# Layer 2's output projection: two more row blocks by the seven-product scheme, and some low parts formed by adding transfers

## The chip, the core and the metric

The kernel runs on one NeuronCore of a Trainium2 chip. Its five engines work side by side: TensorE (PE, matrix products), VectorE (DVE), ScalarE (ACT), GpSimd (POOL) and SyncE (SP, which here only issues transfers). Weights and activations come from HBM by DMA. The metric is the device time of one execution in microseconds (us), the median of several runs.

## The reference, cut to what matters

A trunk of two layers works on 512 tokens of width 2048: a retention layer, then a latent-attention layer, then a final RMSNorm. All is float32. The change lies in the last product of layer 2 and what stands beside it:

```python
def mla_branch(h, pos, w_in, q_norm_g, w_uq, kv_norm_g, w_ukv, w_out):
    ...
    o = causal_block_attention(q, k, v).reshape(B, S, MLA_WIDTH)
    return (jax.nn.silu(g) * o) @ w_out        # (512, 2048) @ (2048, 2048)
...
        x = x + gate * y
    return rmsnorm(x, final_norm_g)
```

## The kernel before

**Layout.** The output is held transposed: 16 blocks `kt` of 128 output rows, each 512 tokens wide. The product runs over 2048 = 16 tiles of 128 input rows. To keep float32 accuracy every operand is split into a high part (a rounding to the matmul's type) and a low part (what is left), and each product is three matmuls: high by high, high by low, low by high. `split` (L134) does that: ScalarE copies with rounding, VectorE subtracts. `load_w` (L138) loads a weight unit into a raw buffer (tag `raw`, three buffers) and splits it into one of three pair buffers, taken in turn (`next_pair`, L231).

**Four stages of the output.** Stage r = 0 forms blocks 0 to 3 and stage r = 1 blocks 4 to 7, both plainly (L2540 to L2549): eight weight units each, a unit being two input tiles by 512 output columns, 24 matmuls of 512 columns. In the first five units of r = 0 lie the last two attention heads (`l2_hooks`, L2384). Then `seven` (from `seven_rows_steps`, L966) forms blocks 8 to 11 by a Strassen-Winograd scheme: inputs in an even and an odd tile, outputs in two pairs of blocks, tokens in two halves of 256, and seven products of half the inner length in place of eight. It has four steps of a first pass (products x, s, z, y) and four of a second (x, y, s); a product is 12 matmuls of 256 columns for each of them. Each step loads its even and odd weights, forms differences on VectorE (L1016 to L1019, L1030) and splits them. The sums of the activations that it multiplies come from `o2_sums` (L2408), for the input pairs u = 0 to 7, in two halves: "s" sums, used in the first pass, and "t" sums, used in the second. For u of 4 and more the t sums are split later by `o2_late_sums` (L2427). At last blocks 12 to 15 are done plainly (`last_load`, `last_prepare`, `last_product`), and the norm and the output follow.

**Evacuation.** `o2_put` (L2471) multiplies a block's sum by the gate, adds the residual that `o2_residual` (L2431) loaded (tag `pp`, five buffers), squares it and adds the squares up. Blocks 4 to 11 wait in the list `waiting`; `put_one` takes one out at set places (`work3`, L2573).

**Buffers and order.** Weights of `seven` and of the last stage are loaded into raw buffers that `turns3[0]` hands out in turn, the tag `raw` (three) and the tag `bw` (two). Their split parts lie in four buffers in turn (`seven_parts`, L2514). `behind(...)` (L463) puts what is written under it after the last instruction issued so far on the named engines: T_ is PE, V_ VectorE, A_ ScalarE, S_ SyncE's queue. Within that freedom a planner, working with assumed durations, fixes the order of each engine's instructions when the kernel is built; on the chip each engine then works in that order, and a waiting instruction holds up what is behind it. In the loop over `seven` (L2579) step j loads step j + 3 and the last stage's units (`loads3`), then the residual of block 4 + j; multiplies; forms late sums at j = 2 and 4; and prepares step j + 2.

Of the kernel before, what the change touches and what calls it, by code (L numbers as in the profile page):

```python
# [9 lines left out]
F32 = mybir.dt.float32  # L10
# [39 lines left out]
def hybrid_trunk_kernel(  # L50
# [59 lines left out]
    def aux(name):  # L110
        return psum.tile([P, T], F32, tag="aux", bufs=4, name=name)
# [22 lines left out]
    def split(src, hi, lo):  # L134
        ACT.copy(hi, src)  # L135
        DVE.tensor_sub(lo, src, hi.bitcast(F32))  # L136

    def load_w(parts, a, b, name, later=None, where=None, halved=False):  # L138

        raw = base.tile([P, a, b], F32, tag="raw", bufs=3, name=f"{name}_raw")  # L140
        for dst, src in parts:
            nc.sync.dma_start(dst(raw), src)
# [2265 lines left out]
    def o2_sums(u):  # L2408

        e, o = (o2_in[u][:, i, :] for i in range(2))  # L2410
        f0 = tmp(f"o2_s{u}f", (P, 2, H))
        if u < 4:
            f1 = tmp(f"o2_t{u}f", (P, 2, H))
        else:
            f1 = late_sums3[u] = l2_tile(*(("sg", 3) if u < 7 else ("rot", 2)), f"o2_t{u}f", (P, 2, H))
        DVE.tensor_add(f0[:, 0, :], e[:, H:], o[:, H:])
        DVE.tensor_sub(f0[:, 1, :], f0[:, 0, :], e[:, :H])
        DVE.tensor_sub(f1[:, 0, :], e[:, :H], e[:, H:])
        DVE.tensor_sub(f1[:, 1, :], o[:, :H], f0[:, 1, :])
        tag, bufs = ("big", 16) if u < 4 else ("k4", 8)  # L2420
        s = sums3[2 * u] = base.tile([P, 2, 2, H], F32R, tag=tag, bufs=bufs, name=f"o2_s{u}")
        split(f0, s[:, :, 0, :], s[:, :, 1, :])
        if u < 4:
            s = sums3[2 * u + 1] = l2_tile("pt", 4, f"o2_t{u}", (P, 2, 2, H), F32R)
            split(f1, s[:, :, 0, :], s[:, :, 1, :])

    def o2_late_sums(u):  # L2427
        s = sums3[2 * u + 1] = base.tile([P, 2, 2, H], F32R, tag="big", bufs=16, name=f"o2_t{u}")
        split(late_sums3.pop(u), s[:, :, 0, :], s[:, :, 1, :])

    def o2_residual(kt):  # L2431
        tag, bufs = ("sg", 3) if kt >= 13 else ("pp", 5)
        o2_res[kt] = l2p.tile([P, T], F32, tag=tag, bufs=bufs, name=f"o2_xr{kt}")
        nc.sync.dma_start(o2_res[kt], x1_d[kt * P : (kt + 1) * P, :])

    def o2_hooks(i):
        l2_hooks.get(i, lambda: None)()
        if i == 5:
            with behind(V_):
                gate_sum()  # L2440
        if 5 < i < 14 and sums3[2 * (i - 6)] is None:
            with behind(V_, A_):
                o2_sums(i - 6)
        if i in (13, 14, 15):
            with behind(S_):
                seven[i - 13].units[0][0]()
# [9 lines left out]
    with behind(V_):  # L2456
        scored(last[0])

    def o2_unit(r, u):
        with ExitStack() as stack:  # L2460
            for ins in o2_first if (r, u) in ((0, 1), (0, 2)) else ():
                stack.enter_context(tc.issue_after(ins))
            wt = load_w([(whole, rows(w_mla_out, u, 2, r * T, T))], 2, T, f"o2_w{r}_{u}")
        if u not in o2_hl:
            o2_parts(u)
        return wt
# [70 lines left out]
        lambda second, u: 0, ((False, 0),),  # L2537
    )

    for r in range(2):  # L2540
        run(
            chunk(
                [(lambda u=u: o2_unit(r, u), [2 * u, 2 * u + 1]) for u in range(KD // 2)],
                [(acc, aux)[r](f"o2_{r}_{b}") for b in range(4)],
                lambda w, ki, kt, b: w_block(w, ki, b), lambda w, ki, kt, b: o2_moving(kt),
                lambda b, ps: o2_out(b, ps)() if r == 0 else waiting.append(lambda: o2_out(4 + b, ps)()),
            ),
            each=lambda i: o2_hooks(r * (KD // 2) + i),
        )  # L2549
# [6 lines left out]
    def last_load(u):  # L2556
        last_raw[u] = turns3[0]([P, 2, T], f"o2_w3_{u}")
        nc.sync.dma_start(last_raw[u], rows(w_mla_out, u, 2, 3 * T, T))
# [16 lines left out]
        7: lambda: (put_one(), put_one(), last_prepare(2)),  # L2575
    }
    with behind(V_, A_):
        seven[1].units[0][1]()
# [207 lines left out]
```

## Time and profile before

| | |
|---|---|
| Median of three runs | 2115.03 us (2114.95 to 2115.57) |
| Profiled execution, its own time | 2114.73 us |
| Span of its trace | 2113.0 us |
| PE busy | 2098.4 us, 99% of the span |
| VectorE, ScalarE, GpSimd busy | 1680.8, 1054.1, 103.8 us |
| Stage r = 0 of the output | PE from about 1920 to 1973.4 us |
| Stage r = 1 | 1973.4 to 2016.9 us |
| `seven` | 2016.9 to 2055.3 us |
| Last blocks, norm, output | 2055.3 to 2113.0 us |

The span is the time from the first to the last instruction of the trace; the execution's own time adds 1.73 us around it. Busy time of PE is modelled and counts pipelined matmuls as overlapping, so the time that a row of matmuls takes is read from the starts of the first and of the next row. In group rows the columns are line, engine, operation, tile written and tiles read, shapes, count, then busy us, mean ns of one, and idle time before them with its cause. In rows in order of time the columns are start, duration, engine, line and operation; a bracket holds the idle time before it.

### The profile page before, as it was taken

The numbers are of one execution on the slowest core, as the hardware profiler recorded it, in microseconds if no ns is written. First come the engines' busy times: TensorE is split into PE (matmuls) and PEld (weight loads), VectorE is DVE, ScalarE is ACT, GpSimd is POOL, SyncE is SP. The second block draws the span as 40 slices with busy tenths as digits, with TensorE's granted clock in tenths as the row PEclk, the third lists the DMA queues.
The fourth block names the chain that finished last, engine by engine and source line by source line (L and its number), as shares of the span: only waits on it lengthen the run. The fifth ranks groups of instructions, "written<-read, shape, count | busy, mean of one in ns | idle before, by whom it ended". The sixth has DMA issues, their size and how long they took to land.

```text
span 2113.0 us, 30423 instructions
## 1 busy us (share of the span) xinstructions
PE 2098.4 (99%) x11268; PEld 1814.2 (86%) x11268; DVE 1680.8 (80%) x2562; ACT 1054.1 (50%) x1626; POOL 103.8 (5%) x177
## 2 busy tenths in 40 slices
PE   8999999999999999999999999999999999999998
PEld 6888898989889888888888888898889999888898
DVE  7999888888888789666777877767978788887675
ACT  6765444444444444434344445345446565665343
POOL 1001010000000000000000000010000000000000
PEclk9999999999999999999999999999999999999999
DMA  9975786868777778755656656753556655455453
GB/s 382 407 281 195 250 276 222 278 216 268 245 259 250 237 237 278 260 188 183 234 170 227 220 184 235 265 178 111 167 186 207 199 166 187 153 188 176 148 166 126
DMA packets 237303, 465.08 MB, mean 220 GB/s; under 512 B 21169, under 2 KB 91857, under 8 KB 233569
## 3 DMA queue, kind: packets, MB, share of 16 engines
q1 hardware_dynamic: 224512, 423.17, 60.5%
q0 software_dynamic: 11920, 38.91, 4.8%
q8 instruction: 88, 1.44, 0.3%
q10 hardware_dynamic: 722, 1.06, 0.2%
q14 instruction: 61, 0.50, 0.1%
HBM read 420.06 MB, written 43.00 MB: 219 GB/s over the span
## 4 chain that ended last, share of the span: by engine, by line
PE 95%; DMA 3%; DVE 1%; ACT 0%; SPq 0%; issue 0%; POOLq 0%; DVEq 0%
PE o L1486 16%; PE x L884 2%; PE x L883 2%; PE y L884 2%; PE y L883 2%; PE s L884 2%; PE s L883 2%; PE x L885 2%; PE s L885 2%; PE y L885 2%; PE o L2607 2%; PE qk L158 2%; PE s_qk L984 2%; PE x_qk L984 2%; PE qk L160 2%; PE qk L159 2%
## 5 line engine op out<-in xcount | busy, mean ns | idle before, releaser
L1486 PE MATMUL o<-o_h,o_p 128*128 128x512 f32 (+1 forms) x1088 | 322.9, 377 | 0.0
L1486 PEld LDWEIGHTS o<-o_h,o_p 128*128 128x128 f32 x1088 | 200.2, 188 | 37.1
L1486 PE MATMUL o<-o_l,o_p 128*128 128x512 f32 (+1 forms) x544 | 204.8, 377 | 0.0
L136 DVE TENSOR_TENSOR o_p<-o_r,o_p 128x1024 fp32r<-128x1024 f32 x64 | 78.1, 1221 | 52.5 <-ACT o_p L135 52.2
L1486 PEld LDWEIGHTS o<-o_l,o_p 128*128 128x128 f32 x544 | 102.3, 188 | 18.2
L1170 DVE SCALAR_TENSOR_TENSOR mod<-mod,c_odd 128x1024 f32<-128x1024 f32 x56 | 67.2, 1219 | 14.9 <-DMA mod<-in_ada_t_dram 14.9
L135 ACT CAST o_p<-o_r 128x1024 fp32r<-128x1024 f32 x64 | 66.7, 1053 | 21.3 <-PE o L1486 7.7
L158 PE MATMUL qk<-hT,qk_p 128*128 128x512 f32 x192 | 75.0, 391 | 0.0
L160 PE MATMUL qk<-hT,qk_p 128*128 128x512 f32 x192 | 74.8, 390 | 0.0
L159 PE MATMUL qk<-hT,qk_p 128*128 128x512 f32 x192 | 74.7, 389 | 0.0
L389 DVE SCALAR_TENSOR_TENSOR aw<-aw,c_all 128x2048 f32<-128x2048 f32 (+1 forms) x37 | 73.2, 1997 | 1.6 <-DMA aw<-in_ada_t_dram 1.4
L1332 ACT ACTIVATE yn<-y,nmr,gn_r 128x512 f32<-128x512 f32 x32 | 22.3, 777 | 67.7 <-DVE nmr L1326 67.7
L159 PE MATMUL o<-o_l,o_w 128*128 128x512 f32 x128 | 49.9, 390 | 0.3 <-DVE o_l L136 0.3
L158 PE MATMUL o<-o_h,o_w 128*128 128x512 f32 x128 | 50.1, 391 | 0.0
L160 PE MATMUL o<-o_h,o_w 128*128 128x512 f32 x128 | 49.9, 390 | 0.0
L1170 DVE SCALAR_TENSOR_TENSOR mod<-mod,c_bm 128x1024 f32<-128x1024 f32 x40 | 48.7, 1218 | 0.0
L448 PE MATMUL g<-hT,g_p 128*128 128x512 f32 x192 | 46.1, 389 | 0.0
L2046 PE MATMUL uv<-ukv_p,kvT 128*128 128x256 f32 x384 | 46.1, 279 | 0.0
L136 DVE TENSOR_TENSOR qk_p<-qk_r,qk_p 128x1024 fp32r<-128x1024 f32 x23 | 27.9, 1222 | 22.1 <-ACT qk_p L135 21.8
L2046 PEld LDWEIGHTS uv<-ukv_p,kvT 128*128 128x128 f32 x384 | 44.9, 189 | 0.1
L2607 PE MATMUL o<-o_h,o_w 128*128 128x256 f32 (+1 forms) x208 | 43.6, 306 | 0.0
L160 PEld LDWEIGHTS qk<-hT,qk_p 128*128 128x128 f32 x192 | 36.0, 188 | 7.8 <-DVE qk_p L136 0.3
(1735 smaller groups left out, 6308.0 us busy)
## 6 DMA issues: line engine op xcount, KB each, us to landing
mod<-in_ada_t_dram SPq DMA_DIRECT2D x96, 512.0 KB, 5.7
o_r<-in_ret_w_out_dram SPq DMA_DIRECT2D x64, 512.0 KB, 5.4
aw<-in_ada_t_dram SPq DMA_DIRECT2D x28, 1024.0 KB, 9.5
mod_gate<-in_ada_t_dram SPq DMA_DIRECT2D x32, 512.0 KB, 5.1
qk_r<-in_ret_w_in_dram SPq DMA_DIRECT2D x48, 256.0 KB, 3.2
qk_r<-qk_d SPq DMA_DIRECT2D x32, 256.0 KB, 5.9
v_r<-v_d SPq DMA_DIRECT2D x32, 256.0 KB, 5.8
sg<-g_d SPq DMA_DIRECT2D x32, 256.0 KB, 6.2
```

What stands on the lines that cost most here:

```text
L136: DVE.tensor_sub(lo, src, hi.bitcast(F32))
L158: PE.matmul(o, lhs[0], rhs[0], start=first and not seeded, stop=False, skip_group_check=seeded)
L159: PE.matmul(o, lhs[0], rhs[1], start=False, stop=False, skip_group_check=seeded)
L160: return PE.matmul(o, lhs[1], rhs[0], start=False, stop=last, skip_group_check=seeded)
L883: PE.matmul(banks[b], a[0], w[0], start=first, stop=False, skip_group_check=True)
L884: PE.matmul(banks[b], a[0], w[1], start=False, stop=False, skip_group_check=True)
L885: PE.matmul(banks[b], a[1], w[0], start=False, stop=True, skip_group_check=True)
L984: PE.matmul(o, w[wp][:, i, b * P : (b + 1) * P], a[ap], start=first and i + b + k == 0, stop=k == 2, skip_group_check=True,)
L1170: DVE.scalar_tensor_tensor(out=aw, in0=aw, scalar=1.0, in1=silu_c[j], op0=ALU.mult, op1=ALU.mult, accum_out=row_sums[piece][:, j, b : b + 1],)
L1486: PE.matmul(o, w[i][:, ki, c0 + b * P : c0 + (b + 1) * P], a[j], start=first and i + j == 0, stop=last and i == 1, skip_group_check=True,)
L2046: PE.matmul(ps[:, (t % 2) * 256 : (t % 2 + 1) * 256], a[i], w[k], start=t % 2 + i + k == 0 and kt == 1, stop=kt == 3 and i == 1, skip_grou ...
L2607: PE.matmul(banks3[b][:, cols], last_w[u][i][:, ki, b * P : (b + 1) * P], o2_moving(2 * u + ki, cols)[j], start=u + ki + i + j == 0, stop= ...
```

## The change

Stage r = 1 keeps only blocks 4 and 5: four weight units of four input tiles by 256 columns. Blocks 6 and 7 go to a second seven-product scheme, `halves7`, made by the new `seven_half_steps`. It splits tokens and inner length as `seven` does, but each half of its outputs is one block, so a product is six matmuls of 256 columns, and its four sums lie in two PSUM banks. Steps of `seven` and `halves7` alternate in the list `turns7` (s0, h0, s1, h1, ... in what follows), but for the last two, which are h7 and then s7. Loading runs three entries ahead and preparing two entries ahead in that list; before it was three and two steps of `seven`.

`split_by_adding` forms a low part in another way: ScalarE writes the high part, then ScalarE writes its negative into the low part's buffer, and GpSimd issues a transfer that adds the source to it. It takes the place of `split` for the weight units u = 2, 3 and 4 of r = 0 (source: the weights in HBM once more) and for the four late t sums, u = 4 to 7 (source: the sums in SBUF). The sums of `o2_sums` move to earlier units (u = 0 at unit 5, 1 and 2 at unit 6, then one at each up to unit 11). Residuals move: 4 and 5 at unit 10, then 6 and 7 at j = 3, and one each at j = 4 to 7, where block 11's goes to the tag `rot`.

```diff
     def o2_late_sums(u):
...
-        split(late_sums3.pop(u), s[:, :, 0, :], s[:, :, 1, :])
+        split_by_adding(late_sums3[u], late_sums3.pop(u), s[:, :, 0, :], s[:, :, 1, :])
     def o2_residual(kt):
-        tag, bufs = ("sg", 3) if kt >= 13 else ("pp", 5)
+        tag, bufs = ("sg", 3) if kt >= 13 else ("rot", 2) if kt == 11 else ("pp", 5)
...
-        if 5 < i < 14 and sums3[2 * (i - 6)] is None:
-            with behind(V_, A_):
-                o2_sums(i - 6)
-        if i in (13, 14, 15):
+        for u in {5: (0,), 6: (1, 2), 7: (3,), 8: (4,), 9: (5,), 10: (6,), 11: (7,)}.get(i, ()):
+            if sums3[2 * u] is None:
+                with behind(V_, A_):
+                    o2_sums(u)
+        if i in (9, 10, 11):
             with behind(S_):
-                seven[i - 13].units[0][0]()
-                if i == 14:
-                    for kt in range(4, 8):
+                turns7[i - 9][0].units[0][0]()
+                if i == 10:
+                    for kt in (4, 5):
                         o2_residual(kt)
-        if i == 15:
+        if i == 11:
             with behind(V_, A_):
                 seven[0].units[0][1]()
...
+    def split_by_adding(added, src, hi, lo):
+        ACT.copy(hi, src)
+        ACT.activation(lo, hi.bitcast(F32), AF.Identity, scale=-1.0)
+        POOL.dma_start(lo, added, accum_op=ALU.add)
     def o2_unit(r, u):
...
-            wt = load_w([(whole, rows(w_mla_out, u, 2, r * T, T))], 2, T, f"o2_w{r}_{u}")
+            kn = 2 * r + 2
+            src = rows(w_mla_out, u, kn, r * T, T // (r + 1))
+            if r == 0 and u in (2, 3, 4):
+                raw = base.tile([P, 2, T], F32, tag="raw", bufs=3, name=f"o2_w{r}_{u}_raw")
+                nc.sync.dma_start(raw, src)
+                wt = two_tiles(None, [P, 2, T], f"o2_w{r}_{u}")
+                split_by_adding(src, raw, *wt)
+            else:
+                wt = load_w([(whole, src)], kn, T // (r + 1), f"o2_w{r}_{u}")
...
+    def seven_half_steps(name, c0, finish):
+        def product(bank, n, u, w, first):
+            for i in range(2):
...
+                for k, (wp, ap) in enumerate(((0, 0), (0, 1), (1, 0))):
+                    PE.matmul(bank, w[wp][:, i], a[ap], start=first and i + k == 0, stop=k == 2, skip_group_check=True)
+        def step(second, u):
+            def load():
...
+                w["raw"] = turns3[0]([P, 2, T], n).rearrange("p e (i n) -> p e i n", i=2)
+                if not second:
+                    for e in range(2):
+                        nc.sync.dma_start(w["raw"][:, e], src[e])
+                else:
+                    nc.sync.dma_start(w["raw"][:, 0], src[1])
+                    nc.sync.dma_start(w["raw"][:, 1, 0].rearrange("p (i n) -> p i n", i=2), src[0, :, :, P:])
+            def prepare():
+                if not second:
+                    DVE.tensor_sub(e1, e1, e0)
+                    DVE.tensor_sub(o1, o1, e1)
+                    DVE.tensor_sub(o0, o0, o1)
+                    hl = seven_parts([P, 2, T], n, ASIDE)
+                    split(r.rearrange("p e i n -> p e (i n)"), *hl)
...
+                else:
+                    DVE.tensor_sub(t3, r[:, 0, :, P:], t3)
+                    hl = seven_parts([P, 3 * H], n, ASIDE)
+                    split(r.rearrange("p e i n -> p (e i n)")[:, : 3 * H], *hl)
...
+    def half_finish(x, s, y, m):
+        DVE.tensor_add(m2, m2, y.unsqueeze(1).to_broadcast([P, 2, H]))
...
+    turns7 = [(steps7[j], j, end) for j in range(8) for end, steps7 in enumerate((seven, halves7))]
+    turns7[14:] = [(halves7[7], 7, 0), (seven[7], 7, 1)]
...
-    for j, step in enumerate(seven):
+    for m, (step, j, end) in enumerate(turns7):
         with behind(S_):
-            if j + 3 < 8:
-                seven[j + 3].units[0][0]()
-            for u in loads3.get(j, ()):
-                last_load(u)
-            if j > 3:
-                o2_residual(4 + j)
+            if m + 3 < len(turns7):
+                turns7[m + 3][0].units[0][0]()
+            if not end:
+                for u in loads3.get(j, ()):
+                    last_load(u)
+                for kt in {3: (6, 7), 4: (8,), 5: (9,), 6: (10,), 7: (11,)}.get(j, ()):
+                    o2_residual(kt)
         with behind(T_):
             step.multiply()
-        with behind(V_, A_):
-            early3.get(j, lambda: None)()
+        if not end:
+            with behind(V_, A_):
+                early3.get(j, lambda: None)()
...
         with behind(V_, A_):
-            if j + 2 < 8:
-                seven[j + 2].units[0][1]()
-            work3.get(j, lambda: None)()
+            if m + 2 < len(turns7):
+                turns7[m + 2][0].units[0][1]()
+            if end:
+                work3.get(j, lambda: None)()
```

More of the change, by code (lines that the diff above doesn't have):

```diff
@@ new lines, in half_finish @@
+    def half_finish(x, s, y, m):
+        m2 = m.rearrange("p (a n) -> p a n", a=2)
+        DVE.tensor_add(m2, m2, y.unsqueeze(1).to_broadcast([P, 2, H]))
+        for j, ps in enumerate((x, s)):
+            parts = list(zip((ps, m2[:, j]), both_halves))
+            waiting.append(lambda kt=6 + j, parts=parts: o2_put(kt, parts)())
+    halves7 = seven_half_steps("o2_1h", T + H, half_finish)
+    turns7 = [(steps7[j], j, end) for j in range(8) for end, steps7 in enumerate((seven, halves7))]
+    turns7[14:] = [(halves7[7], 7, 0), (seven[7], 7, 1)]
@@ L2542, in hybrid_trunk_kernel @@
             chunk(
-                [(lambda u=u: o2_unit(r, u), [2 * u, 2 * u + 1]) for u in range(KD // 2)],
-                [(acc, aux)[r](f"o2_{r}_{b}") for b in range(4)],
+                [
+                    (lambda u=u: o2_unit(r, u), list(range((2 * r + 2) * u, (2 * r + 2) * (u + 1))))
+                    for u in range(KD // (2 * r + 2))
+                ],
+                [(acc, aux)[r](f"o2_{r}_{b}") for b in range(4 - 2 * r)],
                 lambda w, ki, kt, b: w_block(w, ki, b), lambda w, ki, kt, b: o2_moving(kt),
@@ L2577, in hybrid_trunk_kernel @@
     with behind(V_, A_):
-        seven[1].units[0][1]()
-    for j, step in enumerate(seven):
+        turns7[1][0].units[0][1]()
+    for m, (step, j, end) in enumerate(turns7):
         with behind(S_):
-            if j + 3 < 8:
-                seven[j + 3].units[0][0]()
-            for u in loads3.get(j, ()):
-                last_load(u)
-            if j > 3:
-                o2_residual(4 + j)
+            if m + 3 < len(turns7):
[5 more added lines that the diff above has]
+                    o2_residual(kt)
         with behind(T_):
             step.multiply()
-        with behind(V_, A_):
-            early3.get(j, lambda: None)()
+        if not end:
+            with behind(V_, A_):
+                early3.get(j, lambda: None)()
         if j == 3:
```

49 lines of the change are left out of this document (added).

## The prediction, made before the changed kernel was run

> **What bounds the kernel now.** I read the page first: busy times, then the chain of work that ended last.
>
> ```profile
> PE 2098.4 (99%) x11268; PEld 1814.2 (86%) x11268; DVE 1680.8 (80%) x2562; ACT 1054.1 (50%) x1626; POOL 103.8 (5%) x177
> ...
> PE 95%; DMA 3%; DVE 1%; ACT 0%; SPq 0%; issue 0%; POOLq 0%; DVEq 0%
> ```
>
> PE is the bound nearly everywhere: whatever the change adds on other engines costs nothing until PE has to wait, and what it saves on PE is a gain only if PE then does not wait. Next the stretches: stage r = 1, `seven`, and what follows, with the busy times of PE, PE weight loads, VectorE, ScalarE and GpSimd.
>
> ```profile
> 1973.40:2017.10 43.70, 43.70 (x195) 36.21 (x194) 29.64 (x50) 16.56 (x22) 0.00 (x0) 1.00 0.46 147
> 2017.10:2055.30 38.20, 38.20 (x337) 38.20 (x337) 28.11 (x35) 19.64 (x26) 0.00 (x0) 1.00 0.53 166
> 2055.30:2113.00 57.70, 50.34 (x365) 47.09 (x363) 31.96 (x56) 23.51 (x38) 1.41 (x2) 0.97 0.40 137
> ```
>
> In both stages that the change rebuilds PE never stops, at the full clock (1.00), with VectorE busy 68% and 74%. So only the number of matmuls can give time there. The one PE wait of the output stage before this is 0.3 us at its start; the change leaves that unit alone.
>
> **What it removes and adds on PE.** From rows in order of time and the chain:
>
> ```profile
> 1973.41 0.39 PE L158 MATMUL o<-o_h,o_w 128*128 128x512 f32 x1
> ...
> 2016.93 0.28 PE L984 MATMUL x_o<-o_h,o_00e 128*128 128x256 f32 x1
> ...
> 2025.40 1.36 PE z_o L984 x12
> ```
>
> Stage r = 1 is 8 units of 24 matmuls, 192 in 43.52 us, 0.2267 us each. A product of 12 narrow matmuls is 1.36 us, 0.1133 each: exactly half. Blocks 6 and 7 cost 96 wide matmuls (21.76 us); `halves7` costs 28 products of 6 narrow ones, 168 in all (19.04 us). Gain: 2.72 us. By the Trainium skill, *TensorE: Matmul & The Clock Gate*, section "Wait — 56ns, not 53.3ns?", every warm matmul carries some 2.5 ns beside its columns, which speaks against halving them; estimated from its formula the gain would be 96 x 215.8 - 168 x 109.2 ns = 2.37 us. The rows above show no such difference, so 2.72 stands.
>
> **VectorE and ScalarE.** Eight splits of r = 1 become four, three more and four half-sized ones lose their subtraction, and `halves7` adds four times three quarter-sized subtractions with a full split, and four times one with a three-quarter split: nearly even for VectorE in all. What matters is that stage r = 1 now lasts 21.8 us, so the work that filled it has half the time, and that buffers come free in another order. I followed the two places where a load waits for a buffer.
>
> **First place: the fourth unit of r = 1.** In the trace:
>
> ```profile
> 1969.25 1.23 DVE L136 TENSOR_TENSOR o_w<-o_w_raw,o_w 128x1024 fp32r<-128x1024 f32 x1 [4.22 <-ACT o_w L135]
> ...
> 1970.40 1.40 DVE L2477 SCALAR_TENSOR_TENSOR x<-o,gate_c,o_xr 128x512 f32<-128x512 f32 x2
> ...
> 1974.39 0.69 DVE L2489 TENSOR_TENSOR x_ss<-x_ss,x_sq 128x512 f32<-128x512 f32 x1
> ...
> 1978.43 0.41 DVE L2416 TENSOR_TENSOR o_s3f<-o_in 128x256 f32<-128x256 f32 x1
> 1978.77 0.41 DVE L2419 TENSOR_TENSOR o_t2f<-o_in,o_s2f 128x256 f32<-128x256 f32 x1
> ...
> 1979.44 0.68 DVE L136 TENSOR_TENSOR o_s<-o_s2f,o_s 128x512 fp32r<-128x512 f32 x1
> ...
> 2000.26 1.22 DVE L136 TENSOR_TENSOR o_w<-o_w_raw,o_w 128x1024 fp32r<-128x1024 f32 x1 [6.23 <-ACT o_w L135]
> ...
> 2001.41 0.68 DVE L1016 TENSOR_TENSOR o_00e_r<-o_00e_r 128x512 f32<-128x512 f32 x1
> ...
> 2003.46 1.22 DVE L1020 TENSOR_TENSOR o_00e<-o_00e_r,o_00e 128x1024 fp32r<-128x1024 f32 x1
> ...
> 1993.45 0.38 SPq L142 DMA_DIRECT2D o_w_raw<-in_mla_w_out_dram  x1
> ...
> 1999.18 1.05 ACT L135 CAST o_w<-o_w_raw 128x1024 fp32r<-128x1024 f32 x1 [6.49 <-DMA o_w_raw<-in_mla_w_out_dram]
> ...
> 2004.71 0.37 SPq L142 DMA_DIRECT2D o_w_raw<-in_mla_w_out_dram  x1
> ...
> 2008.44 1.05 ACT L135 CAST o_w<-o_w_raw 128x1024 fp32r<-128x1024 f32 x1 [3.74 <-DMA o_w_raw<-in_mla_w_out_dram]
> ...
> 2009.53 1.23 DVE L136 TENSOR_TENSOR o_w<-o_w_raw,o_w 128x1024 fp32r<-128x1024 f32 x1 [3.57 <-ACT o_w L135]
> ```
>
> The eighth unit's load (2004.71) went out when VectorE had read s0's even rows (2003.46 + 1.22): that buffer of tag `raw` was the first free. It was split by 2010.76, and PE wanted it at 2016.93 - 5.44 = 2011.49: 0.7 us to spare. VectorE had been idle for 6.2 us shortly before. In the new order the three `raw` buffers go to s0's even rows, h0 and s1's odd rows before the fourth unit's load, so that waits for the same event. But now VectorE has no idle time ahead of it. From the end of the second unit's split (1970.4) it must do the following; an instruction holds VectorE some 0.08 us less than its row says, since the next starts that much ahead of its end (1978.43 to 1978.77 for a row of 0.41). Four evacuations (0.66 each, and three additions of 0.60), the sums of u = 4, 6 and 7 (four of 0.34 and one of 0.60 each; those of u = 5 fit into the 4.2 us ahead of 1969.25), the third unit's low part (1.14), and s0's three differences (2001.41 to 2003.46) and even split (1.22): 14.7 us, so 1985.1. From issue to cast 3.7 (2004.71 to 2008.44), cast and low part 2.3 (to 2010.76): 1991.1. PE, at 5.44 us a unit, comes to it at 1989.7 and needs the low part in its third matmul, 0.45 later: a wait of 1.0 if VectorE never idles, and 3.0 with the slower landing of the seventh unit (1993.45 to 1999.18). Bounds 0 (sums done ahead) and 3.5. I take the middle, **2.0**.
>
> **Second place: h6, block 4, h7 and s7.** Rows of SyncE's queue, VectorE, ScalarE and the landings:
>
> ```profile
> 2048.82 0.34 SPq L2434 DMA_DIRECT2D o_xr<-x_d  x1
> ...
> 2054.24 0.34 SPq L2434 DMA_DIRECT2D o_xr<-x_d  x1
> ...
> 2054.67 0.90 SPq L2558 DMA_DIRECT2D o_w_r<-in_mla_w_out_dram  x2
> ...
> 2048.04 0.75 DVE L2477 SCALAR_TENSOR_TENSOR x<-o,gate_c,o_xr 128x512 f32<-128x512 f32 x1
> ...
> 2053.47 0.74 DVE L2477 SCALAR_TENSOR_TENSOR x<-o,gate_c,o_xr 128x512 f32<-128x512 f32 x1
> ...
> 2045.99 0.68 DVE L1030 TENSOR_TENSOR o_13e_r<-o_13o_r,o_13e_r 128x512 f32<-128x512 f32 x1
> ...
> 2046.78 0.62 ACT L1033 CAST o_13e<-o_13e_r 128x512 fp32r<-128x512 f32 x1 [1.49 <-DVE o_13e_r L1030]
> ...
> 2047.43 0.69 DVE L1034 TENSOR_TENSOR o_13e<-o_13e_r,o_13e 128x512 fp32r<-128x512 f32 x1 [0.76 <-ACT o_13e L1033]
> ...
> o_11o_r<-in_mla_w_out_dram SPq DMA_DIRECT2D x2, 256.0 KB, 4.1
> ...
> o_11e_r<-in_mla_w_out_dram SPq DMA_DIRECT2D x1, 256.0 KB, 2.8
> ...
> o_13e_r<-in_mla_w_out_dram SPq DMA_DIRECT2D x1, 256.0 KB, 4.3
> ```
>
> Block 9's residual (2048.82) was issued the moment block 4's evacuation (2048.04 + 0.75) gave its `pp` buffer back, block 10's after block 5's, and two weight loads stood behind that (2054.67). Before, only loads of the last stage stand there, wanted much later. In the new order h7's and s7's loads are behind block 9's residual, because loading runs three entries ahead of a list twice as long, and block 4's evacuation stands behind h6's preparation. Count from the start Z of s4 on PE; without waits h5 begins at Z + 10.2, h7 at Z + 18.36 and s7 at Z + 20.4.
>
> - s5: h4's preparation follows the additions that end h3, at about Z + 1.1, its cast ends at Z + 2.3. Then ScalarE has the copies and negations of two late sums (4 x 0.52, from the row of 0.62; half of it new) and s5's odd cast (1.05): Z + 5.5. Low part 1.2: Z + 6.7, wanted at Z + 6.1: 0.6 late. Its even part (0.6) ends at Z + 7.3.
> - s6: its odd rows take the `bw` buffer that s5's odd ones leave at Z + 6.7; 0.4 and 4.0 to land, 2.3 to split: Z + 13.4, wanted at Z + 12.2 + 0.6: 0.5 late (0 to 1.4).
> - h5: difference, cast and low part, sized between the half and the full rows: 0.34 + 0.83 + 0.95 = 2.1, so Z + 9.4. h6's load takes h5's `bw` buffer: 4.1 to land (two transfers, as o_11o) and 2.1: Z + 15.6. Block 4: 0.75. Block 9's residual: 0.4. h7's load 4.1, split 2.1: Z + 22.95; with 0.5 for eight handovers between engines (2004.68 to 2004.71 and the like) Z + 23.45. PE is there at 18.36 + 1.1: h7 waits **4.0**. With landings of 2.8 and nothing late before it the wait is near 0, with landings of 5 us it is 5.8.
> - s7: its even rows take the `raw` buffer that h7 leaves, as the last stage's first two units hold the other two: issue 0.4, landing 3.3 (2.8 to 4.3), then 0.68, 0.62 and 0.69 (2045.99 to 2048.12 in the rows): 5.7 after h7's split, while PE has 2.04 of h7 and 2.72 of s7's x and s: 0.9 late (0 to 1.9).
>
> What is late next: nothing that I find. The last stage's first units are split right behind, while PE itself is later.
>
> **Adding transfers.** The trace has no such transfer. Nearest rows:
>
> ```profile
> L2137 POOL DMA_DIRECT2D o_d<-o x16 | 8.7, 543 | 265.7 <-DVE o L2136 227.7 <-DVE nb L2085 37.9
> ...
> o_d<-o POOLq DMA_DIRECT2D x16, 256.0 KB, 3.9
> ...
> DMA to landing us min/median/max: 5.0/6.8/7.3
> ...
> 1921.54 1.03 ACT L135 CAST o_w<-o_w_raw 128x1024 fp32r<-128x1024 f32 x1
> ...
> 1935.69 0.48 PE L158 MATMUL o<-o_h,o_w 128*128 128x512 f32 x1
> ```
>
> GpSimd issues in 0.54 us; 256 KB land in 3.9 us, in the slowest group (L1081, the third row) in 6.8. I take twice 3.9 for 512 KB read and added, with 13.6 (twice 6.8) as the upper bound and 3.9 as the lower. Unit 2 is cast at 1921.54, its negative ready at 1923.6, the transfer out at 1924.2 and landed by 1932: PE wants it at 1935.69. Units 3 and 4 have more room, the late sums far more. So nothing; if it takes 13.6, unit 2 is 2.1 us late.
>
> **The sum.** -2.72 + 2.0 + 0.6 + 0.5 + 4.0 + 0.9 = +5.3 us. The profiled execution took 2114.73 (span 2113.0 and 1.73 around it), 0.30 under the median; it would be 2120.0, the median **2120.3**. Waits near their upper bounds (3.5, 2.0, 5.0, 1.7) give 2124.5; all at zero 2112.3.
>
> **Rivals.** *The buffers come in time* (not slower): h7's rows are hidden if block 9's residual is out by Z + 18.4 - 4.1 - 2.1 = Z + 12.2, against Z + 16.8 above, and the fourth unit if L1020 ends by 1990.1 - 6.0 = 1984.1, against 1985.1. The gain then stands: 2112.3. For it: PE has no wait in these stages now, and the planner has freedom in the order of the sums. Against: that h7's load stands behind the residual, and block 4 behind h6, is written in the code. *One place only*: -2.72 + 2.0 to -2.72 + 5.8, so 2114.3 to 2118.1. *Late adding transfers*: from a landing of 11.5 us on (1924.2 to 1935.69) unit 2 of r = 0 holds PE up; at 13.6 us 2.1 on top of the sum, 2122.4. That would come if GpSimd were held up in issuing while VectorE works; its 16 issues at 543 ns, next to a VectorE 80% busy, give no sign. The Trainium skill, *SBUF — State Buffer*, section "SBUF: two separate sides", warns that GpSimd cannot write descriptors while a VectorE instruction holds the port that they share; by that rule the time would be this rival's.
>
> **How the numbers follow.** This kernel's measurement tells 0.2% (4.2 us) from no change. Chances: forecast 0.52 (its own range 2117 to 2124.5; 0.46 of it slower), late transfers 0.09 (slower), one place only 0.16 (same), buffers in time 0.20 (same), and 0.03 for a gain over 4.2 us, which no row explains. Slower 0.55, same 0.42, faster 0.03. The range reaches to the hidden case: 2112.0 to 2124.5.
>
> **What would show it.** Right: PE rows of `halves7` at 0.113 us a matmul; a PE idle of 1 to 3 us ahead of r = 1's fourth unit, put down to VectorE's low part, whose load starts at the end of L1020; a PE idle of some 4 us ahead of h7, with SyncE's h7 load right behind block 9's residual, right behind block 4's L2477. Wrong: those loads out earlier, or PE idle at units 2 to 4 of r = 0 released by a transfer.

## The result, and the profile after

The changed kernel takes 2127.68 us (median of 4 runs, 2127.48 to 2128.32), the kernel before, on the same chip, 2114.99 (2114.9 to 2115.57): 12.7 us slower, a ratio of 1.0060 with an interval of 1.0043 to 1.0077. The forecast was 2120.3 with a range up to 2124.5, so its sign is right and its size is not: +5.3 was forecast, +12.7 came.

The profiled execution took 2127.48 us with a span of 2125.7. Its busy times and the chain of waits, from the page of the changed kernel:

```profile
PE 2101.5 (99%) x11340; PEld 1818.3 (86%) x11340; DVE 1688.0 (79%) x2580; ACT 1064.8 (50%) x1640; POOL 112.8 (5%) x184
...
PE 91%; DMA 4%; DVE 2%; issue 1%; ACT 1%; SPq 0%; DVEq 0%; POOLq 0%; POOL 0%; ACTq 0%
```

PE still counts as 99% busy, and is busy 3.1 us longer than before with fewer columns to compute: a first sign that matmuls became slower, not only that PE waited. The three stages in a row, r = 1, the two seven-product streams, and the rest, show where (columns: busy time of PE, PE weight loads, VectorE, ScalarE and GpSimd with their instructions, then the granted clock):

```profile
1973.99:2000.62 26.63, 23.69 (x98) 19.00 (x96) 21.32 (x38) 10.53 (x14) 0.00 (x0) 0.94 0.34 109
2000.62:2066.25 65.63, 61.02 (x506) 59.81 (x504) 41.47 (x56) 30.98 (x42) 4.87 (x4) 0.97 0.63 173
2066.25:2125.70 59.45, 50.73 (x366) 47.20 (x364) 31.66 (x57) 22.91 (x37) 1.42 (x2) 0.95 0.40 137
```

Without any wait r = 1 would be half of its 43.52 us, 21.76, and the two streams the 38.23 us that `seven` took plus the 19.04 of `halves7`, 57.27. So r = 1 lost 4.87 us, the streams 8.36, the last stage 1.61 (59.45 against 57.84), and r = 1 began 0.58 later (1973.99 against 1973.41). That is 15.42; less the 2.72 us that the narrow form saves, 12.7. The waits of PE from 1974 to 2072 (total, times, longest):

```profile
PE o_1h_xs L2567 <- ACT o_1h L135: 3.0, 1, 3.0
PE o L158 <- ACT o_w L135: 2.9, 1, 2.9
PE x_o L984 <- DVE o_12o L1031: 0.8, 1, 0.8
PE o L2723 <- DVE x L2492: 0.6, 1, 0.6
PE x_o L984 <- DVE o_11o L1031: 0.3, 1, 0.3
PE o_1h_xs L2567 <- DVE o_1h L136: 0.3, 1, 0.3
PE y_o L984 <- DVE o_13e L1034: 0.2, 1, 0.2
```

They sit where the forecast put them: the fourth unit of r = 1 (2.9), s5 (o_11o), s6 (o_12o), h7 (3.0 and 0.3) and s7 (o_13e), with one more in the last stage (L2723). Up to s7 they add up to 7.5 us; the forecast had 8.0. What it lacked stands in the granted clock around the two large ones (the same columns as above):

```profile
1990.00:1994.00 4.00, 1.06 (x5) 0.56 (x4) 0.65 (x2) 1.04 (x1) 0.00 (x0) 0.98 0.79 258
1994.00:1998.00 4.00, 4.00 (x12) 3.05 (x11) 2.77 (x5) 1.05 (x1) 0.00 (x0) 0.59 0.42 131
1998.00:2002.00 4.00, 4.00 (x25) 3.50 (x24) 2.30 (x5) 1.05 (x1) 0.00 (x0) 1.00 0.00 0
2054.00:2058.00 4.00, 1.04 (x8) 0.70 (x6) 1.11 (x2) 1.55 (x2) 0.00 (x0) 1.00 0.58 191
2058.00:2062.00 4.00, 3.73 (x19) 3.67 (x19) 3.81 (x4) 2.23 (x3) 0.00 (x0) 0.59 0.23 68
2062.00:2066.00 4.00, 3.78 (x32) 3.58 (x31) 3.13 (x5) 2.37 (x4) 0.00 (x0) 0.98 0.29 59
```

The slice behind each wait of 3 us was granted 0.59 of the clock on average. Slices cut to fit show a clock of one half for 3.41 us each time, with 1.00 on both sides:

```profile
1993.87:1997.28 3.41, 3.41 (x10) 2.56 (x9) 2.19 (x5) 1.05 (x1) 0.00 (x0) 0.50 0.43 132
2058.72:2062.13 3.41, 3.41 (x18) 3.41 (x18) 3.09 (x3) 1.64 (x2) 0.00 (x0) 0.50 0.27 81
```

Rows in order of time show what that does, and confirm the first place's chain:

```profile
1987.56 1.22 DVE L1020 TENSOR_TENSOR o_00e<-o_00e_r,o_00e 128x1024 fp32r<-128x1024 f32 x1
...
1988.80 0.37 SPq L142 DMA_DIRECT2D o_w_raw<-in_mla_w_out_dram  x1
...
1992.31 1.04 ACT L135 CAST o_w<-o_w_raw 128x1024 fp32r<-128x1024 f32 x1 [3.54 <-DMA o_w_raw<-in_mla_w_out_dram]
...
1993.41 0.50 PE L158 MATMUL o<-o_h,o_w 128*128 128x512 f32 x1 [2.94 <-ACT o_w L135]
...
1994.07 0.63 PE L158 MATMUL o<-o_h,o_w 128*128 128x512 f32 x1
...
1994.50 0.63 PE L159 MATMUL o<-o_l,o_w 128*128 128x512 f32 x1
```

The fourth unit's load goes out when L1020 has read s0's even rows, as forecast, and PE resumes 2.94 us after its last matmul. Then a 128x512 matmul starts 0.43 us after the one ahead of it, in place of 0.2267. The second chain, on VectorE, SyncE's queue, ScalarE and PE:

```profile
2049.84 0.96 DVE L136 TENSOR_TENSOR o_1h<-o_1h_r,o_1h 128x768 fp32r<-128x768 f32 x1 [0.95 <-ACT o_1h L135]
...
2050.72 0.74 DVE L2492 SCALAR_TENSOR_TENSOR x<-o,gate_c,o_xr 128x512 f32<-128x512 f32 x1
2051.49 0.34 SPq L2434 DMA_DIRECT2D o_xr<-x_d  x1
...
2051.92 0.39 SPq L2580 DMA_DIRECT2D o_1h_r<-in_mla_w_out_dram  x1
...
2055.95 0.43 DVE L2597 TENSOR_TENSOR o_1h_r<-o_1h_r 128x256 f32<-128x256 f32 x1 [3.09 <-DMA o_1h_r<-in_mla_w_out_dram]
...
2057.34 0.39 PE L2567 MATMUL o_1h_xs<-o_h,o_1h 128*128 128x256 f32 x1 [2.96 <-ACT o_1h L135]
...
2058.33 0.50 PE L2567 MATMUL o_1h_xs<-o_h,o_1h 128*128 128x256 f32 x2 [0.27 <-DVE o_1h L136]
```

h6's low part (2049.84), block 4's evacuation, block 9's residual (L2434), h7's load (L2580) and h7's difference follow one another without a gap other than the landing: the chain of the forecast, link by link.

### The profile page after: what moved, and what is told of

The parts are those of the page before. It is cut to its first block, busy times and chain, and to the rows that moved or that the text cites. A ratio compares the mean times of both kernels' runs of the same rounds, so it can differ in the third digit from the quotient of the medians.

```text
span 2125.7 us, 30645 instructions
## 1 busy us (share of the span) xinstructions
PE 2101.5 (99%) x11340; PEld 1818.3 (86%) x11340; DVE 1688.0 (79%) x2580; ACT 1064.8 (50%) x1640; POOL 112.8 (5%) x184
## 4 chain that ended last, share of the span: by engine, by line
PE 91%; DMA 4%; DVE 2%; issue 1%; ACT 1%; SPq 0%; DVEq 0%; POOLq 0%; POOL 0%; ACTq 0%
PE o L1486 16%; PE x L883 2%; PE x L884 2%; PE y L883 2%; PE s L883 2%; PE x L885 2%; PE y L885 2%; PE s L885 2%; PE s L884 2%; PE y L884 2%; PE qk L158 2%; PE s_qk L984 2%; PE x_qk L984 2%; PE qk L160 2%; PE qk L159 2%; PE y_qk L984 2%
## 5 line engine op out<-in xcount | busy, mean ns | idle before, releaser
L2723 PE MATMUL o<-o_h,o_w 128*128 128x256 f32 (+1 forms) x208 | 43.8, 306 | 0.6 <-DVE x L2492 0.6
L160 PEld LDWEIGHTS qk<-hT,qk_p 128*128 128x128 f32 x192 | 36.0, 188 | 7.9 <-DVE qk_p L136 0.3
L158 PEld LDWEIGHTS qk<-hT,qk_p 128*128 128x128 f32 x192 | 36.0, 188 | 7.8 <-ACT g_st L474 0.5
L448 PEld LDWEIGHTS g<-hT,g_p 128*128 128x128 f32 x192 | 36.0, 188 | 7.5
L159 PEld LDWEIGHTS qk<-hT,qk_p 128*128 128x128 f32 x192 | 36.1, 188 | 7.3
```

The costliest lines, as they stand in the source:

```text
L158: PE.matmul(o, lhs[0], rhs[0], start=first and not seeded, stop=False, skip_group_check=seeded)
L159: PE.matmul(o, lhs[0], rhs[1], start=False, stop=False, skip_group_check=seeded)
L160: return PE.matmul(o, lhs[1], rhs[0], start=False, stop=last, skip_group_check=seeded)
L448: PE.matmul(banks[kind][b], lhs[i], rhs[j], start=kt == 0 and i + j == 0, stop=kt == KD - 1 and late, skip_group_check=True,)
```

## The experiments

Lengths of stages in this section are worked out from the rows of the first matmul of each stage. "To s0" is from the first matmul of r = 1 to s0's first, "streams" from there to the last stage's first, "rest" from there to the end of the span. The kernel before: 43.52, 38.23 and 57.84; the changed kernel: 26.63, 65.63 and 59.45. In these runs the kernel before took 2114.78 to 2115.11 us, so a difference between two experiments is good to some 0.3 us. Stage lengths are those of the one profiled execution of each kernel. The expectations name three theories: A, that each wait costs its length and slower matmuls behind it; B, that the change itself (its transfers, its narrow form) slows the core; C, that a wait moves when it is taken away.

### Block 9's residual behind h7's and s7's odd rows

```
-                for kt in {3: (6, 7), 4: (8,), 5: (9,), 6: (10,), 7: (11,)}.get(j, ()):
+                for kt in {3: (6, 7), 4: (8,), 6: (9, 10), 7: (11,)}.get(j, ()):
```

> Block 9's residual is loaded after h7's and s7's odd rows instead of ahead of them; nothing else differs from the changed kernel. Theory A (two late buffers, and slower matmuls behind each wait): h7's PE wait of 2.96 us falls below 0.5 us, the granted clock stays at 1.00 behind it, and with the wait the slow matmuls of h7 and s7 go, 5 to 6 us in all: 2121.5 to 2123, with the first place's wait (2.94 us) as it was. Theory B (the slow matmuls and the remaining loss come from something else in the change, such as the adding transfers or the narrow form): only the 3 us of the wait come back, 2124.5, and slow rows stay where h7 is. Theory C (the wait moves): the next load in the chain, h6's buffer or s7's even rows, holds PE up in its place, 2126 to 2128.

Measured: 2124.77 us (2123.69 to 2125.22), 2.9 below the changed kernel; streams 63.13 (2.5 less). The granted clock is 1.00 in every 4 us slice from 2044 to 2064, and h7 waits 0.73 and 0.49 us instead of 2.96 and 0.27. So the residual was the link that made this wait long. But the gain is half of A's, and the time is B's (2124.5), though the matmuls at half the clock that B would keep at h7 are gone: 0.50 us of new waiting came at s6 (for its cast) and 0.26 at s7, and the shorter waits cost more than their length. A in kind, with some of C.

### s1's rows behind the fourth unit of r = 1

```
-        if i in (9, 10, 11):
+        if i in (9, 10):
...
-    with behind(V_, A_):
-        turns7[1][0].units[0][1]()
+    with behind(S_, V_, A_):
+        turns7[2][0].units[0][0](), turns7[1][0].units[0][1]()
```

> s1's rows are loaded after the fourth unit of r = 1 instead of ahead of it, so that the unit takes the raw buffer that the third unit leaves; nothing else differs from the changed kernel. Theory A: the wait of 2.94 us ahead of the fourth unit is gone, its load goes out some 11 us earlier (at about 1977 instead of 1988.8), the granted clock stays at 1.00, and r = 1 ends 4.5 to 5 us earlier: 2122.7 to 2123.3, with h7's wait (2.96 us) as it was. Theory B: only the 3 us of the wait come back, 2124.7. Theory C: s1, now loaded when s0's even rows have been read, becomes late itself by 1 us or more, and the time stays at 2125 or above.

Measured: 2121.78 us (2121.09 to 2122.29), 5.9 below. To s0 takes 21.76 us, exactly half of 43.52: all 4.87 us came back, 1.9 more than the wait itself, so B is out here. The time is 0.9 under A's range; 0.7 of that is an earlier start of r = 1 (1973.32 for 1973.99). From the queue of SyncE in this run:

```profile
1976.55 0.37 SPq L142 DMA_DIRECT2D o_w_raw<-in_mla_w_out_dram  x1
1976.97 1.01 SPq L1009 DMA_DIRECT2D o_01e_r<-in_mla_w_out_dram  x2
1987.39 0.88 SPq L1009 DMA_DIRECT2D o_01o_r<-in_mla_w_out_dram  x2
```

The fourth unit's load is 12 us earlier; s1's odd rows took its place in the queue (1987.39) and were still early enough. h7's wait is there, 3.58 us.

### Both

> Both edits together: block 9's residual after h7's and s7's odd rows, and s1's rows after the fourth unit. Theory A: the gains add, -5.5 and -4.8 from 2127.7: 2117 to 2118; what stays above the 2112.3 of a change without any wait are the short waits at s5, s6 and the last stage with the slower matmuls behind them. Theory B: 2121.5. Theory C: 2124 or above, with a new PE wait of over 1 us between 1974 and 2071.

Measured: 2119.16 us (2118.48 to 2121.88); to s0 21.76, streams 62.21, rest 59.16. The two large waits are gone, the clock stays at 1.00, and 8.5 of the 12.7 us are back. No PE wait over 0.8 us is left between 1974 and 2071, but the time is 1 to 2 us above A: the short waits that remain (0.3 at s5, 0.8 at s6, 0.2 and 0.5 at h7, 0.2 and 0.2 at s7, 0.5 in the last stage, 2.7 us) go with 6.3 us of lost time in these two stages (4.94 and 1.32).

### Without adding transfers

```
-        split_by_adding(late_sums3[u], late_sums3.pop(u), s[:, :, 0, :], s[:, :, 1, :])
+        split(late_sums3.pop(u), s[:, :, 0, :], s[:, :, 1, :])
...
-            if r == 0 and u in (2, 3, 4):
+            if False:
```

> The adding transfers undone: the low parts of three units of r = 0 and of the late sums are formed by VectorE's subtraction again; the new order with halves7 stays. Theory A: no PE wait hangs on an adding transfer, so taking them away gives nothing or little: s5's wait of 0.3 us goes, since ScalarE no longer has the negations, and VectorE has 4 subtractions of about 0.65 us more in the last 60 us: 2126.5 to 2129. Theory B (the adding transfers slow the core, by the port that GpSimd and VectorE would share or by their traffic): 2 us or more come back, 2125.5 or less.

Measured: 2125.5 us (2125.27 to 2126.44), 2.2 below the changed kernel: B's number. But the place is A's: r = 1 takes 26.54 us as in the changed kernel, the waits at s5 and s6 are both gone, h7's is 3.4. The next two runs part the two causes.

### Both loads moved, and the late sums by subtraction

The first of the two edits above, on top of both moved loads.

> The two moved loads together (block 9's residual, s1's rows), and the late sums' low parts by VectorE's subtraction again; the three units of r = 0 keep their adding transfers. Theory A (ScalarE's four negations and what queues behind them make s5 and s6 late): the PE waits at s5 (0.3 us) and s6 (0.75 us) go, with the 0.118 us matmuls between them and h7: 2116.5 to 2117.5, against 2119.2 with the adding transfers. Theory B (adding transfers cost nothing on the late sums; the 2.2 us that came back without any of them are from the three units of r = 0): 2119 as with both moved loads, and the waits at s5 and s6 stay.

Measured: 2117.98 us (2117.15 to 2118.41), 1.2 below the run with both loads moved (1.5, if each is counted from its own kernel before); streams 60.97 (62.21). The waits at s5 and s6 went, as A has it, but the time is 0.5 us above A's range, and the slower matmuls between s5 and s6, which A had going with the waits, stayed. In the changed kernel the cause stands in ScalarE's and VectorE's rows (two groups of rows in order of time):

```profile
2035.80 0.61 ACT L2462 CAST o_t<-o_t6f 128x512 fp32r<-128x512 f32 x1
2036.32 0.62 ACT L2462 CAST o_t<-o_t7f 128x512 fp32r<-128x512 f32 x1
2036.84 1.15 ACT L2463 ACTIVATE o_t<-o_t 128x512 fp32r<-128x512 f32 x2
2037.89 1.04 ACT L1028 CAST o_11o<-o_11o_r 128x1024 fp32r<-128x1024 f32 x1
...
2038.96 1.22 DVE L1031 TENSOR_TENSOR o_11o<-o_11o_r,o_11o 128x1024 fp32r<-128x1024 f32 x1 [1.48 <-ACT o_11o L1028]
```

s5's cast (L1028) stands behind the two casts and the two negations of the late sums, and VectorE idles 1.48 us for it. The adding transfer takes a subtraction from VectorE and gives ScalarE a negation, just where ScalarE's next instruction is the one that is late.

### The adding transfers alone, on the kernel before

The diff of the changed kernel for `split_by_adding`, `o2_late_sums` and the units 2 to 4 of r = 0, with all else as before.

> The kernel before (block products for blocks 4 to 7, four by seven products) with the adding transfers alone: three units of r = 0 and the four late sums. Theory A: no PE wait in the three units, and in the stage of the late sums ScalarE has room (1.05 us casts with waits of 1 us and more), so 2114.8 to 2115.5. Theory B (GpSimd's transfers slow VectorE's or ScalarE's work where they run): 2116.5 or more, with VectorE's rows longer beside the transfers.

Measured: 2115.03 us against 2115.1, ratio 1.0000 (0.9990 to 1.0009); to s0 43.52, streams 38.23, and r = 1 begins at 1973.32 (1973.41). Theory A. GpSimd issues each of the three units' transfers in 1.18 to 1.27 us, and 512 KB land in 6.8 to 9.4 us, without a PE wait. So the transfers cost nothing by themselves; the negations do where ScalarE is late.

### A PE idle made on purpose, in the kernel before

```
-        DVE.tensor_sub(lo, src, hi.bitcast(F32))
+        [DVE.tensor_sub(lo, src, hi.bitcast(F32)) for _ in range(times)]
...
-            split(raw, hi, lo)
+            split(raw, hi, lo, 3 if name == "o2_w1_7" else 1)
```

The three runs form the low part of the eighth unit of r = 1 two, three and five times over.

> The kernel before, with the low part of the eighth unit of r = 1 formed twice: 1.15 us less than the run with three times, whose PE idle was 1.99 us and whose stages to s0 took 69.36 us against 65.46. So one PE idle of 0.85 us. Theory A (an idle under 1 us leaves the clock alone): the granted clock stays at 1.00, the stages to s0 take 0.85 and some 0.3 us more, 66.6 us. Theory B (the clock falls behind any idle): a slice of 0.5 to 0.8 and 67.5 us or more.

> The kernel before, with the low part of the eighth unit of r = 1 formed three times over in place of once: 2.3 us more of VectorE ahead of PE's third matmul of that unit, which had 1.2 us to spare, so one PE idle of 1.1 us and nothing else. Theory A (an idle costs its listed length and some 0.3 us of draining and refilling; the clock falls only behind idles of near 3 us): the granted clock stays at 1.00 and the time is 2114.8 + 1.4 = 2116.2. Theory B (any idle makes the matmuls behind it slower for many us): 2117.5 or more.

> The same with the low part formed five times over: 4.6 us more of VectorE, so one PE idle of 3.4 us, the length of the two large waits of the changed kernel. Theory A: the granted clock is near 0.6 for some 3 to 4 us behind it, and the time is 2114.8 + 3.4 + 0.3 + 1.7 = 2120.2. Theory B (the slow matmuls of the changed kernel have another cause, its narrow form or its late weights): the clock stays at 1.00 and the time is 2118.5.

| low part formed | PE idle shown, us | to s0, us | over 43.52 | less the idle | median, us (before) |
| --- | --- | --- | --- | --- | --- |
| twice | 0.55 | 44.36 | 0.84 | 0.29 | 2116.11 (2115.11) |
| three times | 1.99 | 47.42 | 3.90 | 1.91 | 2117.03 (2115.10) |
| five times | 2.74 | 48.17 | 4.65 | 1.91 | 2119.39 (2115.10) |

(In the expectations the same lengths are counted from the last matmul of attention, 21.94 us earlier: 65.46 for 43.52.) The idles came out at 0.55, 1.99 and 2.74 us where 0.85, 1.1 and 3.4 were expected. The clock in the slice behind the idle, of the runs with two and three times:

```profile
2016.00:2020.00 4.00, 4.00 (x23) 3.49 (x22) 0.96 (x1) 0.81 (x1) 0.00 (x0) 1.00 0.19 65
```

```profile
2016.00:2020.00 4.00, 4.00 (x13) 3.11 (x13) 1.54 (x2) 0.16 (x1) 0.00 (x0) 0.68 0.30 99
2015.13:2018.54 3.41, 3.41 (x10) 2.63 (x9) 2.37 (x3) 1.03 (x1) 0.00 (x0) 0.50 0.49 157
```

An idle costs 0.3 us beside its length, and some 1.6 us more once the clock falls, which it did behind 1.99 and 2.74 us but not behind 0.55. The 1.6 us are the fall itself: the clock is at 0.50 for 3.41 us here too (the last line; 0.68 is only the average over a slice that the fall does not fill), and in that time eight wide matmuls start 0.427 us apart in place of 0.2267. A's bound ("only behind idles of near 3 us") is too high; where it lies between 1.2 us, the longest single idle in these traces that left the clock alone (near the start of the kernel), and 1.99 is not shown. Of the ten runs with three times the fastest took 2115.05 us and the slowest 2120.10, a wider spread than that of any other kernel here, so it may be that the clock falls in some executions and not in others, which would account for 1.6 of the 5 us; one execution was profiled (2118.99, 2 us above the median), and this isn't shown. The Trainium skill, *TensorE: Matmul & The Clock Gate*, section "HAM oscillation — how this bites in real kernels", warns of idle gaps over about 3.4 us; the rows here show that less is enough. Its section "What's actually happening" has the array go back to half rate after an idle window that runs on its own, wherever the work stands in it. The traces agree with the half rate (a granted clock of 0.50) and with a fall that doesn't begin with the end of the wait (0.7 us behind it with three times, 1.4 us behind h7's first wait in the changed kernel); how the bound depends on where the idle lies, no run here tests.

### The last stage's loads behind s7's

On top of both moved loads and the subtraction:

```
-    loads3 = {4: (0,), 5: (1, 2), 6: (3,), 7: (4, 5)}
+    loads3 = {6: (0, 1), 7: (2, 3, 4, 5)}
```

> The two moved loads, the late sums by subtraction, and the last stage's first four weight loads behind s7's loads in place of between s6's, h6's and h7's, so that they hold no raw or bw buffer while the seven-product stages still load. Theory A (what is left of the loss are waits for buffers that the last stage's weights hold, each with its draining): the waits at h7 (0.6 and 0.5 us) and s7 (0.3 and 0.2) go, s0 to the last stage takes 57.3 to 58.3 us (60.97 without this edit), and the time is 2114 to 2115.5, level with the kernel before. Theory C (the wait moves): the last stage's units come late, with a PE wait of over 1 us at L2723, 2117 or above.

> The same with the late sums' adding transfers kept. If ScalarE's negations alone made s5 late, and the buffers s6: s5's wait of 0.3 us with its slower matmuls stays, s6's goes, and the time is 0.5 to 1 us above that of the subtraction. If both waits hang on the negations, 1.2 us above, and both stay.

Measured: 2115.89 us with the subtraction (2113.86 to 2117.02; ratio 1.0001, 0.9992 to 1.0010), 2117.69 with the adding transfers (2116.37 to 2118.47). With the subtraction the streams take 58.21 us and no PE wait is listed in them: A for the streams. But the rest takes 60.77, because two waits grew in the last stage, which is C for that stage. From the waits of the run with the subtraction, 1974 to 2072:

```profile
PE o L2723 <- DVE x L2492: 0.9, 1, 0.9
PE o L2723 <- DVE m_o_1h L2641: 0.3, 1, 0.3
```

With the adding transfers s5's wait (0.31) is back, s6's is not, and h7 waits 0.49: the first of the two cases, though 1.8 us and not 1 above (1.3 in the streams of the profiled executions).

### And the second unit of the last stage behind the evacuations

```
-        5: put_one, 6: lambda: (last_prepare(0), last_prepare(1), put_one()),
-        7: lambda: (put_one(), put_one(), last_prepare(2)),
+        5: put_one, 6: lambda: (put_one(), last_prepare(0)),
+        7: lambda: (put_one(), put_one(), last_prepare(1), last_prepare(2)),
```

> As the run before last with the last loads later and the late sums by subtraction, but VectorE evacuates block 5 ahead of the first unit of the last stage, and splits that stage's second unit behind the evacuations of blocks 6 and 7 instead of ahead of them: its split waited 2.75 us for its load at 2053.98 while the evacuations stood behind it. Theory A (the last stage's third and fourth banks wait for VectorE's order alone): the PE waits at L2723 (0.9 and 0.3 us) go or fall under 0.3, and with their draining 1.3 to 1.8 us come back: 2114 to 2114.6, just under the kernel before. Theory C (the second unit is late in its place): a PE wait at L2723 released by o_w of 0.5 us or more, 2116 or above.

Measured: 2113.55 us (2112.28 to 2114.19) against 2114.96: ratio 0.9992 (0.9983 to 1.0001). The waits at L2723 are gone, as A has it; the time is 0.5 us under A's range. The stages of this run:

```profile
1973.91:1995.67 21.76, 21.76 (x97) 18.02 (x96) 20.25 (x37) 10.51 (x14) 0.00 (x0) 1.00 0.40 129
1995.67:2053.88 58.21, 58.21 (x505) 58.05 (x504) 44.13 (x63) 28.87 (x38) 0.00 (x0) 1.00 0.55 173
2053.88:2112.00 58.12, 50.42 (x366) 47.28 (x364) 31.65 (x56) 22.95 (x37) 1.42 (x2) 0.97 0.41 146
```

In the first two stages no PE wait is listed, at the full clock, and the time is 1.4 us under the kernel before, a gain too small to be told from none by this measurement. The two stages take 79.97 us, where the kernel before has 81.75 (43.52 and 38.23): 1.8 of the 2.72 us counted for the narrow form. The other 0.9 went from s5 on, where matmuls come slower (told below). So the narrow form does save time on PE, if not all that was counted, and the order of loads, splits and evacuations had hidden it.

## Why the prediction was right in its sign and wrong in its size

- **The gain (-2.72): right as a count, not all of it kept.** The first `halves7` products of the changed kernel, 12 matmuls from row to row:

```profile
2006.21 0.28 PE L2567 MATMUL o_1h_xs<-o_h,o_1h 128*128 128x256 f32 x1
...
2007.57 0.28 PE L2567 MATMUL o_1h_zy<-o_h,o_1h 128*128 128x256 f32 x1
```

That is 1.36 us, as in `seven`, and r = 1 without its wait takes 21.76 us, half of 43.52. The 2.5 ns for every matmul of the Trainium skill (*TensorE: Matmul & The Clock Gate*, section "Wait — 56ns, not 53.3ns?"), which would leave 2.37, do not show. But the forecast took 1.36 us for every product, and some take 1.41 to 1.44: the first two of `seven`, in the kernel before as well, and those from s5 on in the changed one.

- **First place (2.0): mechanism right, price wrong.** The load starts at the end of L1020, and the idle (2.94) is inside the bounds of 0 to 3.5. It is longer than the middle because all sums of u = 4 to 7 ran behind 1977, those of u = 5 too, which the forecast had put ahead of 1969. The stage lost 4.87.
- **s5 and s6 (0.6 and 0.5): mechanism right, mis-sized.** Their idles are 0.32 and 0.75, so 1.07 for 1.1; with the matmuls behind them, from s5's first matmul to h7's (2039.53 to about 2054.2, 12.24 without waits), they cost 2.4.
- **h7 (4.0) and s7 (0.9): right in place.** h7 lost 4.9 us (6.95 from about 2054.2 to 2061.17, for 2.04) with idles of 2.96 and 0.27; s7 1.0 (5.08 for 4.08) with an idle of 0.22 and the end of the slow clock.
- **Adding transfers at nothing: right for the transfers, half right for the change.** PE never waited for one, and alone they change nothing, so the rival with GpSimd held up is out; they land in 7.4 us (median), between the 3.9 and 13.6 of the bounds, and GpSimd's issue takes 1.2 us where the nearest row had 0.54. But the negations of the late sums, which the forecast counted as 1.04 us of ScalarE ahead of s5's cast, so as the cause of its 0.6, were worth 1.2 and 1.8 us in the two pairs of runs with the buffers in time, and up to 2.2 in the changed kernel (the run without any adding transfer).
- **"What is late next: nothing that I find": wrong.** The last stage's fourth bank waited 0.65 us for block 7's evacuation, behind the preparation of s7 and the last stage's units on VectorE; the rest lost 1.61, some 0.9 of it up to its last product and 0.7 behind that, in the norm and the output, for which no run gives the cause. In the run that put the evacuations first that wait is gone, and the rest is back at 58.12.
- **The rivals.** "The buffers come in time" is what the last experiment makes true by hand, at 2113.6 for 2112.3 (its streams take 58.21 us for 57.27, its rest 58.12 for 57.84). "One place only" is each of the first two experiments, and both were above its 2118.1, for the reason below.

**The step that failed** is the sum, which entered every PE idle at its length. Up to s7 the idles came to 7.5 us where 8.0 were forecast, but r = 1 and the streams lost 13.2 us (4.87 and 8.36). Of the 5.8 us between, the idles made on purpose price 3.8 for the two large ones (1.9 each beside their length) and 1.2 for the four short ones (0.3 each); the slower narrow matmuls told of below are another 0.5, and 0.3 is left over. The rest of the miss is the last stage's 1.6 and 0.6 at the start. The upper end of the range was missed for the same reason: it held longer idles and no slower matmul. (It took 5.0 and 1.7 us for h7 and s7; with the bounds of 5.8 and 1.9 that the prediction gives for them it would have been 2125.5, still too low.) That the idles' total came so near is in part luck: the first place was 0.9 us longer than forecast, h7 and s7 together 1.5 shorter.

The 0.58 us at the start of r = 1 is within what one code shows from run to run: in the four profiles whose code up to there is that of the kernel before, r = 1 begins between 1973.41 and 1974.59 (the low part formed twice). No part of the change has been shown to cause it.

What stays open: from s5 on, the narrow matmuls come 0.1175 us apart and not 0.1133, also at a clock of 1.00. Rows of the changed kernel (12 matmuls each):

```profile
2041.52 1.57 PE L984 MATMUL y_o<-o_t,o_11e 128*128 128x256 f32 x12
2042.93 1.57 PE L984 MATMUL s_o<-o_t,o_11o 128*128 128x256 f32 x12
```

They start 1.41 us apart, where the products of `seven` in the kernel before, from its third on, show 1.36. Over some 110 matmuls, until the clock falls behind h7's wait, that is 0.5 us. The waits alone don't make this pace. In the last experiment no wait is listed at s5; its third and fourth matmul start 0.12 and 0.11 us late, and all behind them up to the last stage come at the slower pace. In the run without adding transfers the same two start as late, and the full pace follows. The kernel before has the first 24 matmuls of `seven` 0.120 us apart, without any wait. No run tells the cause.

## What to carry to other kernels

Where PE is the bound, price a PE wait by what it does to PE, not by its length: measure one made on purpose (work doubled ahead of one operand is enough) at two or three lengths, and read the granted clock in narrow slices behind it. A change that takes 3 us of matmuls out of a stage also takes the time in which other engines loaded and prepared, so list for each load whose buffer it waits for and what stands ahead of it in its queue; five edits with the same matmuls, four of order and one that gave the late low parts back to VectorE, were worth 14 us here. Work moved to a half-busy engine is dear where that engine's next instruction is the late one.

## What the hardware showed that I had not expected

In each of the eight places where the granted clock fell behind a PE wait in these traces, it was 0.50 for 3.41 us and then 1.00 again, with the wait as short as 1.99 us or as long as 3.58. Meanwhile 128x512 matmuls came 0.427 us apart in place of 0.2267, and 128x256 ones 0.213 in place of 0.1133, which costs 1.6 us. The fall began between 0.3 us ahead of the end of the wait and 1.6 us behind it; behind single idles of up to 1.2 us there was none. An idle listed at 0.55 us took 0.84 of PE's time: the listed idle begins at the modelled end of a matmul, 0.16 us later than the next one would have started, and the first matmul behind it held the next up by another 0.11. An accumulating transfer of 512 KB held GpSimd's queue 1.18 to 1.27 us and landed in 6.1 to 9.8 us in the changed kernel; alone, together with the four of 256 KB for the late sums, these transfers left the time unchanged (ratio 1.0000, 0.9990 to 1.0009).
